# A two-layer f32 decoder trunk on one core: moving the down groups of the two-quarter chunk behind the next up group

## The chip, the cores and the metric

The kernel runs on one core of one Trainium2 chip. The metric is the device time of one execution in microseconds. The kernel before took 2059.43 us (median of 3 runs, 2058.87 to 2060.9).

## What is computed

Two decoder layers on a stream of 256 tokens by 2048 features, all in f32. Layer 0 mixes tokens by causal pooling, layer 1 by dilated attention; both end in a gated feed-forward network (FFN) with a causal convolution of width 3, and that is where the change lies:

```
def conv_ffn(h, w_up, conv_w, conv_b, w_down):
    u = h @ w_up                                   # (256, 2048) @ (2048, 2 * 5504)
    up = jnp.pad(u, ((0, 0), (CONV_WIDTH - 1, 0), (0, 0)))
    c = conv_b + up[:, 0:S] * conv_w[0]
    for j in range(1, CONV_WIDTH):
        c = c + up[:, j:j + S] * conv_w[j]
    gate, val = jnp.split(c, 2, axis=-1)
    return (jax.nn.silu(gate) * val) @ w_down      # (256, 5504) @ (5504, 2048)
...
h = layer_norm(DEEPNORM_ALPHA * h + ff, ln2_g[i], ln2_b[i])
```

## The kernel before

**Units.** Nearly all the work of TensorE (PE) is a list of units. A unit is one block of a weight matrix, 512 x 512 (1 MB) or less. SP loads it into one of 3 `raw` buffers; ScalarE (ACT) casts it to a high part `wh` (L82), and VectorE (DVE) subtracts that from the block to get the low part `wl` (L83); both go into one of 4 buffers. PE then multiplies in three partial products (high by high, high by low, low by high), so that f32 accuracy is kept. `run_units` emits unit after unit: first the loads up to 5 units ahead and the splits up to 3 units ahead, then the matmuls of the unit, then what was put off with `later(n, fn)`, which runs `fn` behind the matmuls of the n-th unit from now. Each engine works through its own queue in this order, so what stands on DVE or ACT in front of a unit's split delays that unit.

**The FFN.** The 5504 inner features are cut into quarters 0 to 10 of 512 (the last one of 384). For each quarter q, `up(q, mid, end)` puts two *up groups* on the list, the gate and the value group, of four units each; `mid` and `end` are lists of units that are put between the two and behind them. After a group its banks are added into `u` (`evac`, L577 and L578), and `conv` makes the three taps: tap 2 with the bias on ACT (L586), then `second` and `third`, each an ACT scaling per block (L591) and a DVE addition (L592), which are put off by one and two units. The gate then gets its SiLU (L615, L616). The value is multiplied in (L670), and one unit later `three` splits the product into the tile `gq[q]` (L287, L283), which the down groups take as left operand.

**Down groups.** Quarters are collected in chunks, (0,1,2), (3,4,5), (6,7), (8,9,10). `down(n)` gives four *column groups* for chunk n, one for each 512 output columns, and each takes one block of weights per quarter. A block is multiplied either with eight products (`go_t`, L235 to L237: 24 matmuls of 512 columns), or, where its quarter is listed in `sevens`, by a Strassen scheme with seven: two units, "a" and "b", of 42 matmuls of 256 columns in all (L224 to L226). A block of seven products needs more from DVE and ACT: the split of the block and of the sums of its parts (`split_sums`, L96 to L109), and once per quarter the sums of the left operand (`left_sums`: L645 to L648, and one unit later L654 and L656). In quarters 2, 5 and 7 these sums take a buffer of the pool `hp`, which has five. The column groups of a chunk are put between the up groups of the next quarters, as `mid` and `end`. `free[q]` and `done[q]` hold unit numbers: `free[9]` is the unit behind which `gq[9]` may be made, since its buffer is one that the two-quarter chunk still reads.

**Behind a column group.** DVE takes the sums of the seven products from their banks (`early_post`, L791 to L798) and adds the rest to `HT[c]`, the residual stream with tokens on partitions (L820, L822); GpSimd (POOL) adds the remaining three pieces by accumulating DMAs (L268).

**The turn.** In layer 0 the last chunk is added with features on partitions (`add_last`), and so `HT[c]` must be turned into `H[c]`: `to_features(c)` transposes 32 x 32 blocks on DVE (L777) into a tile of the pool `hp`, and `moves` places them with 16 DMAs on SP's queue (L767), 6, 5 and 5 of them one, two and three units later. The four turns begin 1, 5, 9 and 13 units after the last column group of chunk 2.

**The end of the FFN.** Behind the value group of quarter 10 come the blocks of quarters 8 and 9 for columns 0, then (`turns`) the block of quarter 8 for columns 1, and only then the block of quarter 10 for columns 0, so that three blocks stand between the end of the value group and the first use of `gq[10]`. In layer 1, quarter 9 takes seven products for columns 0 and 2.

Of the kernel before, what the change touches and what calls it, by code (L numbers as in the profile page):

```python
# [21 lines left out]
NF = FF // P  # L22
# [10 lines left out]
def trunk(ctx: ExitStack, tc: tile.TileContext, x, pool_w_in, pool_w_grp, pool_scale, pool_w_out,  # L33
# [18 lines left out]
    units = []  # L52
    state = {"loaded": 0, "split": 0, "done": 0}
# [66 lines left out]
    def later(n, fn):  # L120
        if n == 0:
            fn()
        else:
            pending.append([n, fn])
# [401 lines left out]
    def add_grp(g):  # L526
# [12 lines left out]
             True, 0, 0, after=lambda q: to_tokens(q))  # L539
# [8 lines left out]
    def ffn(lay):  # L548
# [1 line left out]
        gq, gates, xs = {}, {}, {}  # L550

        chunks = [(0, 3), (3, 6), (6, 8), (8, 11)]
        order = {0: (0, 1, 2), 3: (3, 4, 5), 6: (6, 7), 8: (8, 9, 10)}
        every = (0, 1, 2, 3)
        sevens = {1: every, 2: every, 4: every, 5: every, 6: every, 7: every}
        if lay == 1:
            sevens[9] = (0, 2)
        free, done = {}, {}

        def pads():  # L560
# [4 lines left out]
        def evac(ps, nb, mode):  # L565
            fp = pools["ffn"]
            u = pads()

            def tmp():
                return fp.tile([P, T], F32, name="ut", tag="t1", bufs=4)  # L570

            if mode == "x":
                norm_evac(ps, nb, tmp, lambda m: u[:, m, 2:])
                return u
            for m in range(nb):
                t = tmp()
                A.copy(t, ps[m][:, T:])  # L577
                V.tensor_tensor(u[:, m, 2:], ps[m][:, :T], t, OP.add)  # L578
            return u

        def conv(u, blk0, nb, then):
            cv = cvec[lay]
            c = pools["ffn"].tile([P, 4, T], F32, name="c", tag="t4")
            for m in range(nb):
                j = blk0 + m
                A.activation(c[:, m, :], u[:, m, 2:], AF.Identity, scale=cv[:, 2, j:j + 1], bias=cv[:, 3, j:j + 1])  # L586

            def tap(i, to):
                for m in range(nb):
                    j = blk0 + m  # L590
                    A.activation(to[:, m, :], u[:, m, i:i + T], AF.Copy, scale=cv[:, i, j:j + 1])  # L591
                V.tensor_tensor(c[:, :nb], c[:, :nb], to[:, :nb], OP.add)  # L592

            def second():
                tap(1, pools["ffn"].tile([P, 4, T], F32, name="a", tag="t4"))

            def third():
                tap(0, u[:, :, 0:T])
                then(c)

            later(1, second)
            later(2, third)

        def gate_post(q, nb, mode):
            def post(ps):
# [59 lines left out]
        def val_chain(q, nb, mode, ps):  # L665
            u = evac(ps, nb, mode)

            def valued(c):
                s = gates.pop(q)
                V.tensor_tensor(s[:, :nb], s[:, :nb], c[:, :nb], OP.mult)  # L670

                def three():
                    gq[q] = quad_tile("g")
                    split_act(gq[q], s[:, :nb])
                    if q in sevens:
                        left_sums(q, s)

                at(free.get(q, 0), three)

            after(done.get(q, state["done"] + (0 if q in (2, 5, 10) else 1)), lambda: conv(u, NF + 4 * q, nb, valued))  # L680

        def after(u, fn):
            later(max(u - state["done"], 0), fn)
# [4 lines left out]
        def up(q, mid, end):  # L688
            nb = min(4, NF - 4 * q)
            x0 = q == 0  # L690
            mode = "x" if x0 else "ab"
            group(w_up, rows4, 512 * q, nb * P, psrcs if x0 else xsrcs, gate_post(q, nb, mode),
                  mode=mode)
            for g in mid:
                units.extend(g)
            group(w_up, rows4, FF + 512 * q, nb * P, xsrcs, val_post(q, nb, "ab"))
            for g in end:
                units.extend(g)
# [17 lines left out]
        for n in (0, 1):  # L716
            d = down(n, False)
            q = chunks[n + 1][0]
# [3 lines left out]
            if n == 0:  # L722
                up(q + 2, (), ())
        d = down(2, False)
        up(8, d[:1], d[1:2])
        up(9, d[2:3], d[3:])
        free[9] = len(units) - 1
        up(10, (), ())
        mark = len(units)
        if lay == 0:  # L730
            rows = [(512 * q, min(512, FF - 512 * q)) for q in (8, 9, 10)]
# [12 lines left out]
    def to_tokens(q):  # L744
        if q == 0:
            ST["hb"] = hp.tile([P, 4, T], F32, name="hb", tag="h")
        hb = ST["hb"]
        hf = hb.rearrange("p m t -> p (m t)")
        V.transpose(hf.rearrange("p (t m c) -> p m t c", t=2, m=4), H[q].rearrange("p m (t c) -> p m t c", t=2))

        def to():
            HT[q] = hp.tile([P, 4, T], F32, name="ht", tag="h").rearrange("p a t -> p (a t)").rearrange(
                "p (t c) -> p t c", t=2)
            return HT[q].rearrange("p t c -> p (t c)")

        moves(hf, to)
# [17 lines left out]
    def to_features(c):  # L774
        hb = hp.tile([P, 4, T], F32, name="hb", tag="h")
        hf = hb.rearrange("p m t -> p (m t)")
        V.transpose(hf.rearrange("p (m t c) -> p t m c", m=4, t=2), HT[c].rearrange("p t (m c) -> p t m c", m=4))  # L777

        def to():
            H[c] = hp.tile([P, 4, T], F32, name="h", tag="h")  # L780
            return H[c].rearrange("p m t -> p (m t)")

        moves(hf, to)
# [24 lines left out]
    def tm_post(lay, n, c):  # L808
# [2 lines left out]

        def post(t, ps, half=None):
            y = HT[c][:, t, :]
            if lay == 0 and n == 2 and c == 3 and t == 1:
                for q in range(4):
                    later(1 + 4 * q, lambda q=q: to_features(q))
            if half is None and first:
                V.scalar_tensor_tensor(y, y, ALPHA, ps, op0=OP.mult, op1=OP.add)  # L818
            elif half is None:
                V.tensor_tensor(y, y, ps, OP.add)  # L820
            else:
                V.tensor_tensor(y[:, parts[half]], y[:, parts[half]], ps[:, :256], OP.add)  # L822
            if not last:
                return
            if c == 0 and t == 0:
                ST["bn"] = lnp.tile([P, 2, 8, 6], F32, name="bn", tag="bn")
            for i in range(2) if half is None else (half,):
                V.bn_stats(ST["bn"][:, t, 2 * c + i, :], y[:, parts[i]])
            if c == 2 and t == 1:
                for nm, w in (("g", ln2_g), ("b", ln2_b)):  # L830
                    r = rawp.tile([P, 4, 512], F32, name=nm, tag="raw")
                    nc.sync.dma_start(r.rearrange("p a c -> p (a c)"), w[1:2, :].to_broadcast([P, D]))
                    ST[nm] = r
                later(2, early)
            if c == 3 and t == 0:
                finish0()
            if c == 3 and half == 1:
                finish1()
# [233 lines left out]
    with tc.tile_pool(name="pool", bufs=1) as pp:  # L1072
# [5 lines left out]
        for l in range(2):  # L1078
            n = 80 if l == 0 else 64
# [93 lines left out]
```

## Time and profile before

| | us |
|---|---|
| median of 3 runs | 2059.43 |
| the profiled execution | 2059.19 |
| its span, from the first to the last instruction | 2057.4 |
| PE busy | 2033.1 (99%) |
| DVE busy | 1668.2 (81%) |
| ACT busy | 1242.4 (60%) |

The span is 1.8 us less than the time of the same execution. A PE matmul's duration in the profile is longer than the distance to the next one, since matmuls are pipelined; what a group costs is read from the time between the first matmul of it and the first of the next. A row of the view by windows has, for a stretch of time, its length, the busy time of each engine with the number of instructions that touch the stretch, the mean granted clock (PEclk, 1.00 is full), the DMA share and GB/s.

### The profile page before, as it was taken

To read this page: it belongs to the slowest core of one execution; us is meant where nothing else is said; L and a number is where in the kernel's file an instruction comes from. 1 tells how busy PE (TensorE), PEld (TensorE's weight loads), DVE (VectorE), ACT (ScalarE), POOL (GpSimd) and SP (SyncE) were. 2 spreads that over 40 slices of the span, in tenths; PEclk is the share of its full clock that TensorE was granted. 3 is DMA by queue.
4 is the path that set the end of the run, shared out by engine and by line. 5 is a ranking of instruction groups with operands and counts; after the bars stand their busy time and mean duration, and the time that the engine had idled before them with its cause. 6 is when DMAs were issued, how large, how long until landed. Compare 5 with 4: busy or idle time off the path is not lost. (4 is left out here: it accounts for less than half of the span.)

```text
span 2057.4 us, 30875 instructions
## 1 busy us (share of the span) xinstructions
PE 2033.1 (99%) x12388; PEld 1813.7 (88%) x12388; DVE 1668.2 (81%) x2008; ACT 1242.4 (60%) x1649; POOL 75.2 (4%) x112
## 2 busy tenths in 40 slices
PE   9999999999999989999999999999999999989999
PEld 8899988889889879889888888998898888889987
DVE  6859877988988799789756667787888888889988
ACT  6545687666666566656534444487765676566762
POOL 2000000000000101000000000000001001001000
PEclk9999999999999999999999999999999999999999
DMA  8655567657656657775566555557567647647665
GB/s 260 212 192 185 171 213 209 196 177 233 215 174 203 208 162 228 204 214 183 187 198 194 170 178 168 182 188 223 182 194 230 215 159 222 218 134 226 195 211 177
DMA packets 278304, 405.90 MB, mean 197 GB/s; under 512 B 80414, under 2 KB 95668, under 8 KB 277904
## 3 DMA queue, kind: packets, MB, share of 16 engines
q1 hardware_dynamic: 266144, 389.72, 57.2%
q0 software_dynamic: 11584, 13.55, 4.4%
q8 instruction: 97, 1.59, 0.3%
q10 hardware_dynamic: 432, 0.66, 0.1%
q14 instruction: 47, 0.39, 0.1%
HBM read 380.01 MB, written 2.10 MB: 186 GB/s over the span
## 5 line engine op out<-in xcount | busy, mean ns | idle before, releaser
L165 PE MATMUL acc<-xc,wh 128*128 128x512 f32 x3264 | 1150.2, 396 | 0.0
L166 PE MATMUL acc<-xc,wl 128*128 128x256 f32 x3264 | 917.1, 281 | 0.0
L83 DVE TENSOR_TENSOR wl<-raw,wh 128x2048 fp32r<-128x2048 f32 (+2 forms) x326 | 704.9, 2171 | 235.7 <-ACT wh L82 232.1
L82 ACT CAST wh<-raw 128x2048 fp32r<-128x2048 f32 (+2 forms) x326 | 588.7, 1812 | 275.3 <-PE acc L165 136.6
L165 PEld LDWEIGHTS acc<-xc,wh 128*128 128x128 f32 x3264 | 616.7, 189 | 143.5 <-DVE o L1025 0.6
L166 PEld LDWEIGHTS acc<-xc,wl 128*128 128x128 f32 x3264 | 616.1, 189 | 0.1
L96 ACT CAST wh<-raw 128x1024 fp32r<-128x1024 f32 x100 | 101.3, 1050 | 151.5 <-PE acc L165 57.3
L97 DVE TENSOR_TENSOR wl<-raw,wh 128x1024 fp32r<-128x1024 f32 x100 | 118.5, 1221 | 40.1 <-ACT wh L96 40.1
L103 ACT CAST wh<-raw 128x1024 fp32r<-128x1024 f32 x100 | 78.5, 834 | 42.8 <-PE acc L165 36.6
L577 ACT COPY ut<-acc 128x256 f32<-128x256 f32 x164 | 56.8, 371 | 72.4 <-PE acc L166 72.3
L586 ACT ACTIVATE c<-u,cv 128x256 f32<-128x256 f32 x172 | 89.5, 593 | 13.2 <-DVE f L648 8.2
L106 DVE TENSOR_TENSOR wl<-raw,wh 128x1024 fp32r<-128x1024 f32 x100 | 91.1, 954 | 0.0
L268 POOL DMA_DIRECT2D ht<-w x24 | 20.3, 848 | 1846.9 <-DVE ht L818 1126.5
L226 PE MATMUL t<-wh,g 128*128 128x256 f32 x296 | 84.2, 285 | 3.5 <-DVE u L562 3.5
L225 PE MATMUL t<-wl,g 128*128 128x256 f32 x296 | 84.4, 285 | 0.0
L224 PE MATMUL t<-wh,g 128*128 128x256 f32 x296 | 84.2, 284 | 0.0
L237 PE MATMUL t<-wh,g 128*128 128x512 f32 (+1 forms) x211 | 80.9, 383 | 1.0 <-DVE g L283 1.0
L235 PE MATMUL t<-wh,g 128*128 128x512 f32 (+1 forms) x211 | 81.1, 384 | 0.0
L236 PE MATMUL t<-wl,g 128*128 128x512 f32 (+1 forms) x211 | 80.6, 382 | 0.0
L591 ACT ACTIVATE a<-u,cv 128x256 f32<-128x256 f32 x172 | 73.5, 499 | 7.0 <-DVE g L656 7.0
L225 PE MATMUL s<-wl,xs 128*128 128x256 f32 x252 | 72.0, 286 | 3.9 <-DVE wl L97 3.9
L578 DVE TENSOR_TENSOR u<-acc,ut 128x256 f32<-128x256 f32 x164 | 60.0, 416 | 18.4 <-ACT ut L577 18.4
(274 smaller groups left out, 3473.3 us busy)
## 6 DMA issues: line engine op xcount, KB each, us to landing
raw<-in_ffn_w_up_dram SPq DMA_DIRECT2D x160, 1024.0 KB, 4.9
raw<-in_ffn_w_down_dram SPq DMA_DIRECT2D x80, 1024.0 KB, 5.2
raw<-in_pool_w_out_dram SPq DMA_DIRECT2D x16, 1024.0 KB, 5.0
raw<-in_shared_w_k_dram SPq DMA_DIRECT2D x16, 1024.0 KB, 5.1
raw<-in_attn_w_q_dram SPq DMA_DIRECT2D x16, 1024.0 KB, 5.3
raw<-in_shared_w_v_dram SPq DMA_DIRECT2D x16, 1024.0 KB, 5.7
raw<-in_attn_w_o_dram SPq DMA_DIRECT2D x16, 1024.0 KB, 5.0
raw<-in_pool_w_in_dram SPq DMA_DIRECT2D x12, 1024.0 KB, 5.3
```

Source lines behind the costliest of these rows:

```text
L82: A.copy(wh[i][:, s], r[:, s])
L83: V.tensor_tensor(wl[i][:, s], r[:, s], wh[i][:, s].bitcast(F32), OP.subtract)
L96: A.copy(h[:, :, n], r[:, :, n])
L97: V.tensor_tensor(l[:, :, n], r[:, :, n], h[:, :, n].bitcast(F32), OP.subtract)
L106: V.tensor_tensor(l[:, k, n], r[:, k, n], h[:, k, n].bitcast(F32), OP.subtract)
L165: PE.matmul(ps[m], h[:, k, c], q[:, k, :, :T], start=st, stop=False)
L166: PE.matmul(ps[m][:, :T], l[:, k, c], q[:, k, 0, :T], start=False, stop=sp and not shifted)
L224: PE.matmul(to, xh, h[:, k, n], start=opens and kk == 0, stop=False)
L225: PE.matmul(to, xh, l[:, k, n], start=False, stop=False)
L226: PE.matmul(to, xl, h[:, k, n], start=False, stop=ends and kk == 1)
L235: PE.matmul(to, xh, h[:, k, c], start=j == 0 and k == 0, stop=False)
L586: A.activation(c[:, m, :], u[:, m, 2:], AF.Identity, scale=cv[:, 2, j:j + 1], bias=cv[:, 3, j:j + 1])
```

## The change

- In both layers the four column groups of chunk 2 (quarters 6 and 7) are placed later: behind the value group of quarter 8 instead of behind its gate group, and so on, the last one between the gate and the value group of quarter 10 instead of behind quarter 9. `free[9]` moves with the last of them.
- In layer 0 quarter 7 takes eight products instead of seven, and comes first in each column group of its chunk.
- In layer 0 the turn of each column `c` begins three units after its own column group.
- The value of quarter 10, in both layers, gets its second and third tap at once instead of one and two units later.

```
-        order = {0: (0, 1, 2), 3: (3, 4, 5), 6: (6, 7), 8: (8, 9, 10)}
+        order = {0: (0, 1, 2), 3: (3, 4, 5), 6: (6, 7) if lay == 1 else (7, 6), 8: (8, 9, 10)}
         every = (0, 1, 2, 3)
-        sevens = {1: every, 2: every, 4: every, 5: every, 6: every, 7: every}
+        sevens = {1: every, 2: every, 4: every, 5: every, 6: every}
         if lay == 1:
-            sevens[9] = (0, 2)
+            sevens.update({7: every, 9: (0, 2)})
...
-        def conv(u, blk0, nb, then):
+        def conv(u, blk0, nb, then, quick=False):
...
-            later(1, second)
-            later(2, third)
+            for n, fn in ((1, second), (2, third)):
+                later(0 if quick else n, fn)
...
-            after(done.get(q, state["done"] + (0 if q in (2, 5, 10) else 1)), lambda: conv(u, NF + 4 * q, nb, valued))
+            after(done.get(q, state["done"] + (0 if q in (2, 5, 10) else 1)), lambda: conv(u, NF + 4 * q, nb, valued, q == 10))
...
         d = down(2, False)
-        up(8, d[:1], d[1:2])
-        up(9, d[2:3], d[3:])
-        free[9] = len(units) - 1
-        up(10, (), ())
+        up(8, (), d[:1])
+        up(9, d[1:2], d[2:3])
+        up(10, d[3:], ())
+        free[9] = len(units) - 5
...
-            if lay == 0 and n == 2 and c == 3 and t == 1:
-                for q in range(4):
-                    later(1 + 4 * q, lambda q=q: to_features(q))
+            if lay == 0 and n == 2 and t == 1:
+                later(3, lambda: to_features(c))
```

How the change moves instructions is shown at three places on DVE. The digits in a name are buffer numbers; the number behind `wl`, `wh` and `raw` is that of the unit. From line 816 on, line numbers are one less in the changed program.

**Layer 0, where the first column group of chunk 2 is prepared.** `c_6327` is the gate of quarter 7 and `g_...` its `gq[7]`. Before:

```order
L592 TENSOR_TENSOR c_6804<-c_6804,u_6630 128x1024
L670 TENSOR_TENSOR c_6327<-c_6327,c_6804 128x1024
L97 TENSOR_TENSOR wl145_6925<-raw144_6764,wh145_6924 128x4x256 x2
L283 TENSOR_TENSOR g_6962<-c_6327,g_6962 128x4x256
L645 TENSOR_TENSOR f_6968<-c_6327 128x256
L646 TENSOR_TENSOR f_6968<-f_6968,c_6327 128x256
L647 TENSOR_TENSOR f_6968<-c_6327 128x256
L648 TENSOR_TENSOR f_6968<-c_6327,f_6968 128x256
L104 TENSOR_TENSOR raw146_6874<-raw146_6874 128x2x256
L106 TENSOR_TENSOR wl146_6976<-raw146_6874,wh146_6975 128x4x256
```

And changed:

```order
L592 TENSOR_TENSOR c_6804<-c_6804,u_6630 128x1024
L670 TENSOR_TENSOR c_6327<-c_6327,c_6804 128x1024
L83 TENSOR_TENSOR wl145_6923<-raw145_6822,wh145_6922 128x2048
L283 TENSOR_TENSOR g_6958<-c_6327,g_6958 128x4x256
L83 TENSOR_TENSOR wl146_6964<-raw146_6876,wh146_6963 128x2048
L562 MEMSET u_6999 128x4x2
L578 TENSOR_TENSOR u_6999<-acc_6828,ut_7001 128x256
L578 TENSOR_TENSOR u_6999<-acc_6829,ut_7004 128x256
L578 TENSOR_TENSOR u_6999<-acc_6830,ut_7007 128x256
L578 TENSOR_TENSOR u_6999<-acc_6831,ut_7010 128x256
L83 TENSOR_TENSOR wl147_7016<-raw147_6920,wh147_7015 128x2048
L83 TENSOR_TENSOR wl148_7061<-raw148_6961,wh148_7060 128x2048
```

Units 144 to 147 were the column group (two blocks of seven products each), split around the making of `gq[7]`; now they are the value group of quarter 8, with plain splits, the left sums of quarter 7 are gone, and the column group begins with unit 148.

**Layer 1, behind the value group of quarter 10.** `u_18651` and `u_18517` are that group's `u`; the `L97` of the first row ends the split of quarter 9's block for columns 0; `wl403` and `wl399` belong to the block of quarter 8 for columns 1, `wl404` and `wl400` to that of quarter 10 for columns 0. Before:

```order
L97 TENSOR_TENSOR wl402_18620<-raw401_18507,wh402_18619 128x4x256 x2
L616 TENSOR_TENSOR c_18540<-u_18496,c_18540 128x768
L562 MEMSET u_18651 128x4x2
L578 TENSOR_TENSOR u_18651<-acc_18513,ut_18653 128x256
L578 TENSOR_TENSOR u_18651<-acc_18514,ut_18656 128x256
L578 TENSOR_TENSOR u_18651<-acc_18515,ut_18659 128x256
L83 TENSOR_TENSOR wl403_18669<-raw403_18577,wh403_18668 128x2048
L592 TENSOR_TENSOR c_18662<-c_18662,a_18698 128x768
L83 TENSOR_TENSOR wl404_18706<-raw404_18617,wh404_18705 128x1536
L592 TENSOR_TENSOR c_18662<-c_18662,u_18651 128x768
L670 TENSOR_TENSOR c_18540<-c_18540,c_18662 128x768
```

And changed:

```order
L97 TENSOR_TENSOR wl398_18488<-raw397_18382,wh398_18487 128x4x256 x2
L562 MEMSET u_18517 128x4x2
L578 TENSOR_TENSOR u_18517<-acc_18388,ut_18519 128x256
L578 TENSOR_TENSOR u_18517<-acc_18389,ut_18522 128x256
L578 TENSOR_TENSOR u_18517<-acc_18390,ut_18525 128x256
L592 TENSOR_TENSOR c_18528<-c_18528,a_18532 128x768
L592 TENSOR_TENSOR c_18528<-c_18528,u_18517 128x768
L670 TENSOR_TENSOR c_18258<-c_18258,c_18528 128x768
L83 TENSOR_TENSOR wl399_18545<-raw399_18449,wh399_18544 128x2048
L283 TENSOR_TENSOR g_18574<-c_18258,g_18574 128x3x256
L83 TENSOR_TENSOR wl400_18580<-raw400_18485,wh400_18579 128x1536
```

The taps and the product moved ahead of the two splits.

**Layer 0, the first turn.** `ht_2837` is `HT[0]`. Before, it stands among the splits of quarter 10's up groups:

```order
L820 TENSOR_TENSOR ht_3471<-ht_3471,t0_8022 128x512
L822 TENSOR_TENSOR ht_3471<-ht_3471,t1_8023 128x256
L83 TENSOR_TENSOR wl175_8164<-raw175_8085,wh175_8163 128x1536
L777 STREAM_TRANSPOSE hb_8194<-ht_2837 128x2x4x128
L83 TENSOR_TENSOR wl176_8199<-raw176_8115,wh176_8198 128x1536
```

And changed:

```order
L107 TENSOR_TENSOR raw156_7325<-raw156_7325 128x2x256
L108 TENSOR_TENSOR raw156_7325<-raw156_7325 128x2x256
L109 TENSOR_TENSOR raw156_7325<-raw156_7325 128x2x256
L777 STREAM_TRANSPOSE hb_7450<-ht_2837 128x2x4x128
L97 TENSOR_TENSOR wl157_7455<-raw156_7325,wh157_7454 128x4x256 x2
```

It now stands one column group after its own, inside the split of the next group's seven-product block.

## The prediction

> **What bounds the kernel now.** I read the page first, then who waits for whom on PE, then the view by windows at each place where PE waits.
>
> ```profile
> span 2057.4 us, 30875 instructions
> PE 2033.1 (99%) x12388; PEld 1813.7 (88%) x12388; DVE 1668.2 (81%) x2008; ACT 1242.4 (60%) x1649; POOL 75.2 (4%) x112
> ```
>
> ```profile
> PE s L225 <- DVE wl L106: 4.8, 2, 2.4
> PE s L225 <- DVE wl L97: 3.9, 4, 1.6
> PE acc L165 <- DVE g L283: 3.7, 1, 3.7
> PE t L226 <- DVE u L562: 3.5, 2, 2.1
> PE t L237 <- DVE g L283: 1.0, 1, 1.0
> ```
>
> PE sets the end: it is busy nearly throughout, and an engine of 81% can only cost time where PE has to wait for it. The waits inside the program are these five rows (us in total, times, longest), and the releaser is DVE in all of them. Where do they lie? The windows below run from the first matmul of a group to the first of the next, except the last four.
>
> ```profile
> 686.75:692.34 5.59, 5.59 (x26) 4.52 (x25) 4.76 (x7) 1.84 (x3) 0.00 (x0) 1.00 0.41 157
> 702.24:724.72 22.48, 22.48 (x130) 19.64 (x129) 17.13 (x24) 13.33 (x23) 2.58 (x3) 1.00 0.62 180
> 724.72:743.83 19.11, 12.24 (x87) 11.42 (x85) 18.30 (x27) 13.80 (x23) 0.00 (x0) 0.91 0.26 85
> 766.31:776.22 9.91, 9.91 (x86) 9.91 (x85) 8.53 (x13) 9.71 (x14) 0.00 (x0) 1.00 0.46 158
> 841.00:906.97 65.97, 62.25 (x346) 54.09 (x345) 50.83 (x53) 35.70 (x44) 2.58 (x3) 0.97 0.84 236
> 1835.88:1855.60 19.72, 14.34 (x87) 13.34 (x86) 18.91 (x27) 14.43 (x23) 0.00 (x0) 0.74 0.30 99
> 1878.07:1887.97 9.90, 9.90 (x86) 9.90 (x85) 7.77 (x11) 9.70 (x14) 0.00 (x0) 1.00 0.37 122
> 1952.72:1986.46 33.74, 33.74 (x194) 29.51 (x193) 27.87 (x35) 20.56 (x29) 2.58 (x3) 1.00 0.76 241
> ...
> 739.19:742.60 3.41, 2.86 (x13) 2.86 (x14) 2.73 (x3) 3.41 (x6) 0.00 (x0) 0.50 0.17 43
> 892.78:896.19 3.41, 0.69 (x4) 0.61 (x5) 3.25 (x4) 2.63 (x2) 0.00 (x0) 1.00 0.84 238
> 896.19:899.60 3.41, 3.41 (x13) 2.92 (x12) 2.88 (x4) 0.00 (x0) 0.00 (x0) 0.50 0.98 270
> 2002.80:2004.20 1.40, 0.39 (x2) 0.00 (x0) 1.40 (x3) 0.81 (x1) 0.00 (x0) 1.00 0.60 230
> ```
>
> A column group of two seven-product blocks takes 9.91 us (84 matmuls; a window's count has those at its edges too), except the first of chunk 2 in each layer: 19.11 and 19.72 us, where DVE is busy 18.3 and 18.9 us. A block of eight products takes 5.59 us, an up group 22.48 us, that is 22.48 / 64 = 0.351 us for each pair of a 512 and a 256 column matmul. The stretch from 841.00 has quarter 10's two groups (2 x 4 x 12 pairs) and the first five blocks behind them (16, 16, 16, 12, 16), 172 pairs or 60.42 us, and took 65.97: 5.55 too long. The clock is part of all this: behind a wait it stood at 0.50 for 3.4 us, or, in 1835.88 to 1855.60, for longer (mean 0.74).
>
> **Part 1: the column groups of chunk 2 begin an up group later.** What makes the first of them late is DVE's queue:
>
> ```profile
> 726.58 2.35 DVE L97 TENSOR_TENSOR wl<-raw,wh 128x1024 fp32r<-128x1024 f32 x2
> 728.86 1.22 DVE L283 TENSOR_TENSOR g<-c,g 128x1024 fp32r<-128x1024 f32 x1
> ...
> 731.46 0.69 DVE L104 TENSOR_TENSOR raw<-raw 128x512 f32<-128x512 f32 x1
> ...
> 735.25 0.69 DVE L109 TENSOR_TENSOR raw<-raw 128x512 f32<-128x512 f32 x1
> 735.86 0.69 DVE L656 TENSOR_TENSOR xs<-f,xs 128x512 fp32r<-128x512 f32 x1
> ...
> 737.48 1.08 DVE L578 TENSOR_TENSOR u<-acc,ut 128x256 f32<-128x256 f32 x3
> 738.47 2.35 DVE L97 TENSOR_TENSOR wl<-raw,wh 128x1024 fp32r<-128x1024 f32 x2
> ```
>
> From 726.58 to 740.82 it is back to back: splitting a block of seven (L104 to L109 with L97, some 6.8 us from 731.46), making `gq[7]` with its sums (2.6 us from 728.86, 1.3 us from 735.86), adding up the gate of quarter 8, all in the 9.9 us that PE needs. With the up group in front, the making of `gq[7]` falls beside 22.5 us of PE work whose four plain splits take 4 x 2.2 us of DVE. I add DVE's work in that group for layer 1: splits of its last unit and of the three pieces ahead 2.2 + 4.5 + 2.3 + 4.5, additions, product and sums of banks 4.8, together 18.3 of 22.5 us. So DVE gains 4 us there and adds to its lead, the time between the end of a split and PE's use of it. Both first groups come down to what the others take. Layer 1: 19.72 - 9.90 = 9.82 us gained. Layer 0 has the other block type: 19.11 - (5.59 + 9.91 / 2) = 8.57 gained.
>
> Behind them the pattern "value group, column group, gate group, column group" is that of before, shifted, where no row waits. New is the last place, between the two short groups of quarter 10: 33.74 / 2 = 16.87 us each. A cycle of one short group and one column group gives PE 26.8 us. DVE's work in it is, from a full cycle of before:
>
> ```profile
> 1920.38:1952.72 32.34, 32.34 (x214) 29.54 (x213) 29.91 (x35) 22.25 (x34) 2.59 (x3) 1.00 0.65 195
> ```
>
> 29.9 us less a quarter of four splits (4 x 0.54, from 2.29 and 1.75 us for blocks of 2048 and 1536) and of the tap work (about 1.2) is 26.5 us: as much as PE has. That holds without a wait only because DVE begins ahead; one short cycle takes from the lead rather than adding the 2.4 us of a full one. I put it at nothing. If the lead doesn't suffice, each of some six units is late by up to 1 us.
>
> **Part 2: quarter 7 in layer 0 with eight products.** PE pays 5.59 - 4.95 = 0.64 us per block. The first column group has it above; three more make +1.92. DVE has one plain subtraction of 2.29 us instead of 6.8, and no left sums: cover for part 3.
>
> **Part 3: the turn behind each group.** No PE work. Four transposes (1.24 us) move into DVE's queue ahead of the L97 of a seven-product block, and with each 16 DMAs on SP (some 0.6 us each to issue) ahead of weight loads. What can hold them is the accumulation into `HT[c]`:
>
> ```profile
> 754.50 0.85 POOL L268 DMA_DIRECT2D ht<-w  x1 [38.59 <-ACT wh L103]
> 755.03 2.05 POOL L268 DMA_DIRECT2D ht<-u  x2
> ...
> 760.81 2.43 DVE L97 TENSOR_TENSOR wl<-raw,wh 128x1024 fp32r<-128x1024 f32 x2
> ```
>
> ```profile
> DMA to landing us min/median/max: 3.3/4.7/8.5
> ...
>   DMA h<-hb: 4.9, 2
> ```
>
> The first rows are the timeline, the others the views of lines L268 and L777.
>
> Here the column group ended at 743.83, POOL issued from 754.50 to 757.1, and a median landing is at 762, 18 us after the end. DVE reaches the turn no sooner than the buffer of the split ahead comes free, two units (11.2 us) after the end, plus 4.5 us of that split, so 15.7 us: it would stand about 2 us. In this row the L97 was done at 763.2 and PE used it from 768.5, 5 us later, and the plain block of quarter 7 adds to that. I cost the part at nothing; without that cover it is some 2 us per column. It takes away the 4.9 us that DVE waited for one turn's DMAs before the next.
>
> **Part 4: the taps of quarter 10 at once.** In layer 0 this removes the 5.55 us: three blocks, 16.8 us, follow the group, and the chain of copies, taps, product and split needs about 9 us now that nothing stands between. In layer 1 it removes the 1.0 us at 2002.80, but the chain now stands ahead of the split of quarter 8's block for columns 1:
>
> ```profile
> 1987.38 2.35 DVE L97 TENSOR_TENSOR wl<-raw,wh 128x1024 fp32r<-128x1024 f32 x2
> 1989.65 0.95 DVE L616 TENSOR_TENSOR c<-u,c 128x768 f32<-128x768 f32 x1
> 1990.54 0.41 DVE L578 TENSOR_TENSOR u<-acc,ut 128x256 f32<-128x256 f32 x1
> ...
> 1994.40 2.29 DVE L83 TENSOR_TENSOR wl<-raw,wh 128x2048 fp32r<-128x2048 f32 x1 [2.79 <-ACT wh L82]
> ```
>
> ```profile
> 1990.98 1.59 ACT L586 ACTIVATE c<-u,cv 128x256 f32<-128x256 f32 x3 [1.75 <-DVE u L578]
> 1992.48 1.89 ACT L82 CAST wh<-raw 128x2048 fp32r<-128x2048 f32 x1
> 1994.27 1.31 ACT L591 ACTIVATE a<-u,cv 128x256 f32<-128x256 f32 x3
> 1995.48 1.47 ACT L82 CAST wh<-raw 128x1536 fp32r<-128x1536 f32 x1
> ```
>
> Before, that block's `wl` was done 6.15 us after the first L578 (1996.69 less 1990.54), and PE used it at 1997.2. Two tap rounds on ACT, 1.21 us each (1994.27 to 1995.48), now come before its cast: 8.6 us. The group ended at 1986.46 and the block is due 5.59 + 4.95 us later, its `wl` at 10.8. The first L578 stood at 4.1; without L616 (now earlier) 3.2, which makes PE wait 1.0 us. But the sums of quarter 9 (3.9 us of DVE) move from quarter 10's gate group into its value group; if none of it is absorbed, the L578 stands at 7.1 and the wait is 4.9. I take a third of that, 4.5, since this group has the lead of a plain stretch: a wait of 2.4 us.
>
> **The sum.** Layer 0: -8.57 + 1.92 - 5.55 = -12.2. Layer 1: -9.82 - 1.0 + 2.4 = -8.4. Together -20.6: the profiled execution's 2059.19 us becomes 2038.6. It lies 0.2 us under the median, so the forecast against the runs is **2038.8 us**.
>
> **The clock.** In 892.78 to 896.19 PE was busy 0.69 of 3.41 us, and the next 3.41 us ran at 0.50; the 1.0 us wait at 2002.80 left the clock at 1.00. So a wait of about 2.7 us inside one such window is enough, and costs 1.7 us more. [...]
>
> **The rivals.**
> - *No new wait in layer 1.* The lead absorbs the chain: 2.4 us less, 2036.4. For it: the block was in time before by 0.5 us. Against it: 2.4 us more of ACT work ahead of its cast.
> - *The long wait in layer 1.* Nothing of quarter 9's sums is absorbed: 4.9 us and 1.7 for the clock, 2038.8 + 4.2 = 2043.0. For it: the 26.5 of 26.8 us just before.
> - *DVE becomes the bound around the last column group*, in both layers: six units late by up to 1 us in layer 1, half of this in layer 0, and the clock twice: 2038.8 + 9 + 3.4 = 2051. Against it: leads of several us in the rows of before.
> - *The waits only move*: the first column groups still find DVE behind, and stand at 19 us. The gain is then part 4 less part 2, 1 to 4 us: 2055 to 2059. Against it: the 18.3 of 22.5 us.
> - *The turns hold DVE*, slower. The place is L777 ahead of the L97. It decides when the accumulation lands so late that the lead is used up: about 2 us of standing, plus 5 of lead at each column. To lose the 12.2 us of layer 0 and 8.4 of layer 1, each of four holds has to cost PE over 5.2 us, so land 10 us later than the median. With 6.5 us each, 26 in all: 2064. For it: DVE works in order, and SP's loads queue behind the turn's DMAs too. Against it: the largest landing is 8.5 us, 3.8 over the median.
>
> **How the numbers follow.** Forecast 0.50 (2036.5 to 2041), no new wait 0.13, long wait 0.15, DVE the bound 0.10, waits move 0.05, turns hold 0.07. Below the forecast only the first rival lies, less about 1.5 us of spread: 2034.5. Upward the range takes the long wait and half of the DVE case: 2047. 0.2% is 4.1 us, about what a measurement of this kernel can tell from no change. Faster are the first four and half of the fifth, 0.89; the same the other half, 0.03; slower the last, and a small part for what I do not see, 0.08.
>
> **What would show it.** Right: the first column group of chunk 2 takes 10.5 us in layer 0 and 9.9 in layer 1 with PEclk 1.00; the other three of layer 0 take 10.5; no wait of `acc` for `g`; one wait of PE in layer 1 for the `wl` of L83 behind quarter 9's first block, 1 to 5 us. Wrong: a wait for L97 behind a transpose, waits for `wl` in quarter 10's groups, or a clock of 0.50 in the FFNs. The prediction fails as a whole if the lead of DVE in the value group of quarter 8 doesn't form.

## The result and the profile after

| | before | changed |
|---|---|---|
| median of the runs, us | 2059.15 (2056.26 to 2060.9, 4 runs) | 2041.12 (2040.18 to 2042.79, 4 runs) |
| span of the profiled execution, us | 2057.4 | 2041.0 |
| mean granted clock | 0.995 | 0.998 |

The ratio is 0.9915, with a 95% interval of 0.9898 to 0.9932: the changed kernel is faster by 18.0 us in the medians. The page of its profile and PE's waits (us in total, times, longest):

```profile
span 2041.0 us, 30664 instructions
PE 2029.8 (99%) x12316; PEld 1805.3 (88%) x12316; DVE 1648.8 (81%) x1973; ACT 1235.0 (61%) x1634; POOL 75.2 (4%) x112
```

```profile
PE t L236 <- DVE wl L83: 1.9, 1, 1.9
PE acc L168 <- ACT wh L82: 1.8, 1, 1.8
...
PE t L235 <- ACT wh L82: 0.8, 1, 0.8
...
PE acc L166 <- DVE wl L83: 0.4, 1, 0.4
```

All five rows of before are gone, those for `g` among them. The L168 row lies at 8 us, in the start of the kernel, which the change does not touch; it is 1.8 us here, between 0.2 and 1.6 in some of the kernels below and absent in others. The other three rows are layer 1. The places of the prediction in the view by windows (length, then busy PE, PEld, DVE, ACT, POOL, then PEclk, DMA share, GB/s):

```profile
748.35:758.86 10.51, 10.51 (x68) 9.46 (x67) 6.88 (x9) 8.89 (x12) 0.00 (x0) 1.00 0.61 201
841.72:852.23 10.51, 10.51 (x69) 9.46 (x67) 7.24 (x10) 7.91 (x11) 0.00 (x0) 1.00 0.67 156
852.23:895.79 43.56, 43.56 (x250) 38.05 (x249) 34.27 (x38) 24.01 (x28) 2.58 (x3) 1.00 0.86 256
1847.21:1857.13 9.92, 9.92 (x86) 9.92 (x85) 9.16 (x14) 8.29 (x15) 0.00 (x0) 1.00 0.29 94
1857.13:1880.34 23.21, 22.79 (x130) 19.64 (x129) 22.98 (x25) 14.24 (x19) 2.59 (x3) 1.00 0.79 244
1966.35:1977.88 11.53, 10.71 (x68) 9.42 (x66) 8.99 (x14) 8.70 (x15) 0.00 (x0) 1.00 0.58 204
1977.88:2006.82 28.94, 27.05 (x108) 21.56 (x109) 27.39 (x33) 12.83 (x11) 0.00 (x0) 0.94 0.58 200
```

**Layer 0.** The first two rows are the first and the last column group of chunk 2: 10.51 us each, with PE busy from end to end. The third row is the stretch from the last column group to the end of the fifth block behind quarter 10, without a wait. Against before, the first column group is worth 10.51 - 19.11 = -8.60, the other three 3 x (10.51 - 9.91) = +1.8, and the wait for `gq[10]` -5.55: 12.3 us less.

**Layer 1.** The fourth row is the first column group, 9.92 us in place of 19.72: -9.80. The gate group of quarter 9 behind it (fifth row) takes 23.21 in place of 22.48: +0.7, the 0.4 of L166 in the waits. The 1.0 us wait for `gq[10]` is gone. The last two rows hold the new wait: the first blocks of quarters 8 and 9 behind the value group of quarter 10 take 11.53 us in place of 5.59 + 9.91 / 2 = 10.54, since PE stops at their end for the `wh` of quarter 8's block for columns 1 (the 0.8 of L235); then it waits for that block's `wl` and runs at a mean clock of 0.94. The same stretch of PE's work takes 25.11 us in a kernel below that has no wait there. So this place costs 1.0 + 3.8 = 4.8 us. Layer 1 gains 9.80 - 0.7 + 1.0 - 4.8 = 5.3 us.

Together 12.3 + 5.3 = 17.6, less 1.1 us by which the FFN of layer 0 began later in this execution (the start of the kernel): 16.5 against the 16.4 us between the two spans. The profiled execution of the changed kernel is the longest of its four (2042.79 us), so the spans show 1.6 us less gain than the medians.

### The profile page after: what moved, and what is told of

It reads as the page before. It is cut to its first block, busy times and chain, and to the rows that moved or that the text cites. A ratio compares the mean times of both kernels' runs of the same rounds, so it can differ in the third digit from the quotient of the medians.

```text
span 2041.0 us, 30664 instructions
## 1 busy us (share of the span) xinstructions
PE 2029.8 (99%) x12316; PEld 1805.3 (88%) x12316; DVE 1648.8 (81%) x1973; ACT 1235.0 (61%) x1634; POOL 75.2 (4%) x112
## 5 line engine op out<-in xcount | busy, mean ns | idle before, releaser
L166 PE MATMUL acc<-xc,wl 128*128 128x256 f32 x3264 | 915.9, 281 | 0.4 <-DVE wl L83 0.4
L83 DVE TENSOR_TENSOR wl<-raw,wh 128x2048 fp32r<-128x2048 f32 (+2 forms) x330 | 713.8, 2171 | 238.8 <-ACT wh L82 233.0
L82 ACT CAST wh<-raw 128x2048 fp32r<-128x2048 f32 (+2 forms) x330 | 596.5, 1814 | 279.7 <-PE acc L165 136.5
L166 PEld LDWEIGHTS acc<-xc,wl 128*128 128x128 f32 x3264 | 615.4, 189 | 0.9 <-DVE wl L83 0.7
L96 ACT CAST wh<-raw 128x1024 fp32r<-128x1024 f32 x92 | 93.3, 1050 | 146.5 <-PE acc L165 69.4
L97 DVE TENSOR_TENSOR wl<-raw,wh 128x1024 fp32r<-128x1024 f32 x92 | 108.8, 1219 | 38.6 <-ACT wh L96 38.5
L103 ACT CAST wh<-raw 128x1024 fp32r<-128x1024 f32 x92 | 72.2, 834 | 49.8 <-PE acc L165 42.9
L236 PE MATMUL t<-wl,g 128*128 128x512 f32 (+1 forms) x243 | 93.9, 387 | 1.9 <-DVE wl L83 1.9
L235 PE MATMUL t<-wh,g 128*128 128x512 f32 (+1 forms) x243 | 94.6, 389 | 0.8 <-ACT wh L82 0.8
L237 PE MATMUL t<-wh,g 128*128 128x512 f32 (+1 forms) x243 | 94.0, 387 | 0.0
L106 DVE TENSOR_TENSOR wl<-raw,wh 128x1024 fp32r<-128x1024 f32 x92 | 83.7, 951 | 0.2 <-ACT wh L103 0.2
L578 DVE TENSOR_TENSOR u<-acc,ut 128x256 f32<-128x256 f32 x164 | 60.2, 414 | 21.0 <-ACT ut L577 21.0
L225 PE MATMUL t<-wl,g 128*128 128x256 f32 x272 | 76.4, 281 | 0.0
L224 PE MATMUL t<-wh,g 128*128 128x256 f32 x272 | 76.4, 281 | 0.0
L226 PE MATMUL t<-wh,g 128*128 128x256 f32 x272 | 76.3, 281 | 0.0
L591 ACT ACTIVATE u<-u,cv 128x256 f32<-128x256 f32 x172 | 73.4, 499 | 0.0
```

The source lines that it names most:

```text
L82: A.copy(wh[i][:, s], r[:, s])
L83: V.tensor_tensor(wl[i][:, s], r[:, s], wh[i][:, s].bitcast(F32), OP.subtract)
L96: A.copy(h[:, :, n], r[:, :, n])
L97: V.tensor_tensor(l[:, :, n], r[:, :, n], h[:, :, n].bitcast(F32), OP.subtract)
L106: V.tensor_tensor(l[:, k, n], r[:, k, n], h[:, k, n].bitcast(F32), OP.subtract)
L166: PE.matmul(ps[m][:, :T], l[:, k, c], q[:, k, 0, :T], start=False, stop=sp and not shifted)
```

## The experiments

Medians are set against runs of the kernel before on the same chip; ratios have 95% intervals. "Part" is one of the four parts of the prediction. Lines of diffs are against the kernel that the text names.

**Part 4 alone: the taps of quarter 10 at once, everything else as before.** Against the kernel before:

```
-            later(1, second)
-            later(2, third)
+            for n, fn in ((1, second), (2, third)):
+                later(0 if quick else n, fn)
...
-conv(u, NF + 4 * q, nb, valued))
+conv(u, NF + 4 * q, nb, valued, q == 10))
```

> The kernel before with part 4 alone: the value of quarter 10 gets its second and third tap at once, in both layers; column groups, quarter 7 and turns as before. Theory (each part works by itself; in layer 1 the taps ahead of the split of quarter 8's block for columns 1 are what makes that block late, by 8.6 us from the first L578 to its wl): layer 0 loses its 5.55 us; in layer 1 the first L578 stands some 4.1 us behind the value group, as before, so the block is ready at 12.7 against 10.8 us, a wait of 1.9 us in the place of the 1.0 us for g; in all 2059.2 - 5.5 + 0.9 = 2054.6 us. Rival (the new wait in layer 1 comes from the moved sums of quarter 9 and the short groups, not from the taps): no wait there, 2059.2 - 5.5 - 1.0 = 2052.7 us, and PE has no wait behind quarter 10 in either layer.

Measured: 2055.22 us (9 runs) against 2060.03, ratio 0.9978 [0.9968, 0.9988]. PE's waits:

```profile
PE s L225 <- DVE wl L106: 4.8, 2, 2.4
...
PE t L236 <- DVE wl L83: 1.7, 1, 1.7
...
PE shift L362 <- DVE S L345: 0.9, 1, 0.9
```

Both waits for `gq[10]` are gone and the first column groups are as late as before (L106). The wait for `wl` in layer 1 is there without the other parts: the three taps ahead of the split make it. It is 1.7 us here and, with all four parts, 1.9 behind a stop of 0.8 for `wh`. The prediction's reason for a longer one, the sums of quarter 9 that part 1 moves into quarter 10's value group, fits that: the first L578 stands 3.96 us behind the group here (1986.91 less 1982.95) and 5.25 us with all four parts. In layer 1 the two kernels differ in part 1 alone, but no run has the sums by themselves. The L362 row is new too: the last split ahead of DVE's sums for the norm waits 1.70 us for ACT's cast. Why the cast is late there was not tested.

**Part 1 alone: the column groups of chunk 2 an up group later.** Against the kernel before:

```
-        up(8, d[:1], d[1:2])
-        up(9, d[2:3], d[3:])
-        free[9] = len(units) - 1
-        up(10, (), ())
+        up(8, (), d[:1])
+        up(9, d[1:2], d[2:3])
+        up(10, d[3:], ())
+        free[9] = len(units) - 5
```

> The kernel before with part 1 alone: the column groups of chunk 2 an up group later in both layers; quarter 7 of layer 0 with seven products, turns and taps as before. Theory: the first column group takes 9.9 to 10.6 us in both layers (8.5 to 9.2 us gained in layer 0, about 9.1 in layer 1), while the wait for the g of quarter 10 stays and grows by 1 to 2 us in each layer because the sums of quarter 9 now lie in its value group: 2059.2 - 9 - 9.1 + 3 = about 2044 us. Rival (without the eight products of quarter 7, DVE is behind in layer 0): the column groups of layer 0 stand at 12 us and more with waits for L97, and the time is 2049 us or more.

Measured: 2051.42 us (4 runs), ratio 0.9955 [0.9941, 0.997]. The number is the rival's, but not by its mechanism: each of the eight column groups takes 9.9 us. PE's waits and the DVE row behind the first of them:

```profile
PE acc L399 <- DVE S L348: 5.1, 1, 5.1
PE acc L165 <- DVE g L283: 4.7, 1, 4.7
PE t L237 <- DVE g L283: 1.4, 1, 1.4
```

```profile
944.57 1.42 DVE L318 TENSOR_TENSOR h<-h,acc 128x256 f32<-128x256 f32 x4 [4.95 <-DMA h<-hb]
```

The two waits for `gq[10]` stay, as they must without part 4. The first row is new: before, the four turns ran from the last column group through quarter 10's up groups; now that the last column group comes later, the fourth turn (13 units behind it) ends inside the last chunk. DVE stands 4.95 us for its DMAs before it can add to `H[3]`, and the sums for the norm (`S`) and PE's use of them (L399) wait in turn. In the view by windows the stretch from the block in which PE stops to the end of the chunk is

```profile
936.69:969.27 32.58, 27.19 (x199) 26.09 (x198) 26.30 (x31) 18.49 (x24) 0.00 (x0) 0.90 0.48 155
```

The changed kernel needs 5.75 + 18.29 = 24.04 us for it (its rows stand with the next run), 8.5 less. That is most of what part 1 alone gives back of its gain.

**Part 3 undone: the turns spread as before, behind the last column group.** Against the changed kernel:

```
-            if lay == 0 and n == 2 and t == 1:
-                later(3, lambda: to_features(c))
+            if lay == 0 and n == 2 and c == 3 and t == 1:
+                for q in range(4):
+                    later(1 + 4 * q, lambda q=q: to_features(q))
```

> The changed kernel with part 3 alone undone: the four turns of layer 0 start 1, 5, 9 and 13 units after the last column group again. Theory (part 3 has a price only together with part 1: with the column groups later, turns counted from the last of them end inside the last chunk): the DMAs of the fourth turn land after quarter 10's last block is done, DVE stands for them, and PE waits for the sums of the layer norm (L399 for S) by 5 us or more, then runs at half clock for 3.4 us; the column groups and quarter 10 in layer 0 are as in the changed kernel. 2041.1 + 8.7 (what the same place lost with part 1 alone) = 2050 us, up to 2055. Rival (the prediction as it was costed: part 3 is free either way): 2041 us, and no wait for S.

Measured: 2047.28 us (4 runs) against 2059.18, ratio 0.9949 [0.9935, 0.9964]: 6.2 us over the changed kernel. PE's waits, windows (the block of the last chunk where PE stops, and what follows), and DVE:

```profile
PE acc L399 <- DVE S L348: 4.3, 1, 4.3
```

```profile
930.91:941.09 10.18, 5.91 (x50) 5.70 (x49) 7.01 (x14) 2.28 (x5) 0.00 (x0) 1.00 0.71 222
941.09:963.06 21.97, 21.21 (x149) 20.57 (x150) 20.74 (x21) 16.52 (x21) 0.00 (x0) 0.84 0.40 133
```

```profile
914.68 1.25 DVE L777 STREAM_TRANSPOSE hb<-ht 128x1024 f32<-128x1024 f32 x1 [1.15 <-DMA h<-hb]
...
937.97 1.42 DVE L318 TENSOR_TENSOR h<-h,acc 128x256 f32<-128x256 f32 x4 [3.07 <-DMA h<-hb]
```

and the same stretch of the changed kernel:

```profile
932.61:938.36 5.75, 5.75 (x51) 5.75 (x50) 5.58 (x11) 3.37 (x8) 0.00 (x0) 1.00 0.89 322
938.36:956.65 18.29, 18.29 (x151) 17.99 (x149) 17.16 (x17) 13.75 (x17) 0.00 (x0) 1.00 0.39 122
```

10.18 + 21.97 against 5.75 + 18.29: 8.1 us at this one place, with a clock of 0.84 in the second stretch. The mechanism is the theory's; the median is 2.7 us under its 2050, and the rival without a wait for `S` fell. The last turn begins at 914.68, and DVE has its DMAs at 937.97, 23 us later. This execution is the longest of the four (2050.47 us), and part of the 8.1 may be its own. So part 3 is worth 6.2 us in the medians once part 1 is made, by a place at the very end of the layer.

**Parts 2 and 3 undone: quarter 7 of layer 0 with seven products, the turns as before.** Against the kernel with part 3 undone, above:

```
-        order = {0: (0, 1, 2), 3: (3, 4, 5), 6: (6, 7) if lay == 1 else (7, 6), 8: (8, 9, 10)}
+        order = {0: (0, 1, 2), 3: (3, 4, 5), 6: (6, 7), 8: (8, 9, 10)}
...
-        sevens = {1: every, 2: every, 4: every, 5: every, 6: every}
+        sevens = {1: every, 2: every, 4: every, 5: every, 6: every, 7: every}
...
-            sevens.update({7: every, 9: (0, 2)})
+            sevens[9] = (0, 2)
```

> The changed kernel with parts 2 and 3 undone (quarter 7 of layer 0 has seven products again; the four turns come 1, 5, 9 and 13 units behind the last column group of chunk 2, as before the change); parts 1 and 4 stay. To be set beside the run with part 3 alone undone (2047.28 us), which differs from it in quarter 7 only, and beside the run with the turns three units apart (2063.01), which differs in the distance of the turns only. Theory: eight products in quarter 7 cost PE 4 x 0.6 us and are worth only the cover that they give; with the turns four units apart nothing needs it but the first column group's 0.8 us wait, so this is 2047.3 - 2.5 + 0.8 = 2045.6 us, the four column groups of layer 0 take 9.9 us, and the wait for S in the last chunk stays. The loss of the other run then came from the distance of the turns alone: there DVE stood 7.05 and 6.59 us for one turn's DMAs ahead of the next one's transpose. Rival: the blocks of seven leave DVE without a lead for the taps of quarter 10, whose product is then late whatever the turns do: 2049 us or more, with a wait of acc for g in layer 0.

Measured: 2047.8 us (2044.72 to 2050.35, 6 runs) against 2060.01, ratio 0.9938 [0.9926, 0.995]. The four column groups take 9.9 us, and no wait for `g` is left: the rival's mechanism fell. The waits:

```profile
PE acc L399 <- DVE S L348: 4.4, 1, 4.4
...
PE acc L166 <- DVE wl L83: 1.1, 2, 0.5
...
PE shift L362 <- DVE S L345: 0.9, 1, 0.9
```

Of the 2.5 us that the seven products save, some 0.5 go to a wait behind the first column group (one of the two in the second row; the other is layer 1's) and 0.9 to the wait at L362, which the theory left out. At L362 the last split ahead of the sums for the norm again waits for ACT's cast (1.63 us); the run with part 3 alone undone has the same turns and no such wait, so what makes it is open. In the runs the two kernels can't be told apart: with the turns as before, part 2 is worth nothing that could be measured.

**The same with the turns three units apart**, beginning 1, 4, 7 and 10 units behind the last column group (`1 + 3 * q` in the line above), so that they end sooner.

> The changed kernel with quarter 7 of layer 0 at seven products again, in the old order (6, 7); since its sums then hold the fifth buffer until the last column group, the turns start after that group, 1, 4, 7 and 10 units behind it. Theory (the eight products are there to free the buffer, not to spare DVE): column groups 9.9 us instead of 10.5, 2.6 us less for PE, with a wait of 0.4 to 1 us behind the first group as in layer 1; the turns, three units apart, make DVE stand for the DMAs of the one before, which gives back 1 to 6 us, and PE doesn't wait for S at the end: 2040 to 2045 us. Rival (DVE needs the relief): the column groups of layer 0 take 11 us or more with waits for wl, and the time is over 2046 us.

Measured: 2063.01 us (9 runs), ratio 1.0019 [1.0008, 1.0029]: 15.2 us more than with four units, and the theory's number fell. The time is the rival's, but its mechanism isn't: the column groups of layer 0 take 9.9 us here too. PE's waits and DVE:

```profile
PE shift L362 <- DVE S L345: 8.4, 1, 8.4
PE acc L399 <- DVE S L348: 3.0, 1, 3.0
PE acc L165 <- DVE u L578: 2.3, 1, 2.3
...
PE acc L165 <- DVE g L283: 1.5, 1, 1.5
```

```profile
858.79 1.24 DVE L777 STREAM_TRANSPOSE hb<-ht 128x1024 f32<-128x1024 f32 x1
...
877.55 1.25 DVE L777 STREAM_TRANSPOSE hb<-ht 128x1024 f32<-128x1024 f32 x1 [7.05 <-DMA h<-hb]
...
898.40 1.25 DVE L777 STREAM_TRANSPOSE hb<-ht 128x1024 f32<-128x1024 f32 x1 [6.59 <-DMA h<-hb]
...
916.59 1.25 DVE L777 STREAM_TRANSPOSE hb<-ht 128x1024 f32<-128x1024 f32 x1 [6.18 <-DMA raw<-in_ffn_w_down_dram]
```

The last five DMAs of the first of these turns, in SP's timeline:

```profile
871.07 3.26 SPq L767 DMA_DIRECT2D h<-hb  x5
```

This third part goes out until 874.3, three units behind the turn, and the next transpose, three units on, must wait until it has landed (1.9 to 6.7 us from issue to landing for these DMAs, median 4.3). DVE works in order and stands 7.05 and 6.59 us. Ahead of the fourth transpose it stands another 6.18; the view puts that down to a weight load, which SP issued (912.55) right behind the third turn's last DMAs (until 912.46). Everything behind these transposes is late: the sums of banks (L578), the making of `gq[10]` (L283), the additions for the norm (8.4 us of PE at L362). Four units left 4.9 us of standing in two waits in the kernel before and one wait of 1.5 us in the run above, which differs from this one in nothing else. An up group between two turns, as in the changed kernel, leaves one of 2.6:

```profile
  DMA ht<-u: 2.6, 1
```

This is the view of the transposes (L777) of the changed kernel; what it waits for there is the accumulation into `HT[c]`, and no row names the DMAs from `hb`. The rival of the prediction in which the turns hold DVE is thus real, at another place: it is the distance between two turns that decides, not the landing of the accumulation.

**Layer 1 with the taps of quarter 10 spread as before** (part 4 in layer 0 alone). Against the changed kernel:

```
-conv(u, NF + 4 * q, nb, valued, q == 10))
+conv(u, NF + 4 * q, nb, valued, q == 10 and lay == 0))
```

> The changed kernel, but in layer 1 the taps of quarter 10 come one and two units later again; layer 0 as changed. Theory: the wait for quarter 8's block for columns 1 (1.0 us for wh, 2.1 for wl, and 3.4 us at half clock, 4.8 in all) goes, since cast and split stand ahead of the taps again: 0.7 us of wait for that wl at most, and the wait for the g of quarter 10 comes back at 1 to 2.5 us, so 2041.1 - 4.8 + 2.5 = 2038.8 us (2037 to 2040). Rival (DVE is the bound around the short groups): the block of quarter 8 still waits 2 us or more, and with the g wait the time is 2041 us or more.

Measured: 2038.28 us (4 runs), ratio 0.9895 [0.9878, 0.9912], against 0.9915 of the changed kernel. PE's waits:

```profile
PE t L237 <- DVE g L283: 1.4, 1, 1.4
...
PE t L236 <- DVE wl L83: 0.6, 1, 0.6
```

As the theory had it: two waits of 1.4 and 0.6 us at full clock (the mean over the execution is 1.000) in place of 2.7 us and half clock. By the medians part 4 thus costs 2.8 us more in layer 1 than the wait that it removes; the intervals of the two ratios overlap from 0.9898 to 0.9912, and the waits and the clock are the better evidence.

**Layer 1 with the three taps at once, but one unit later.** Against the changed kernel:

```
-            after(done.get(q, state["done"] + (0 if q in (2, 5, 10) else 1)),
+            after(done.get(q, state["done"] + (0 if q in (2, 5) or q == 10 and lay == 0 else 1)),
```

> The changed kernel, but in layer 1 all three taps of quarter 10 stand one unit later, at once, so behind the split of quarter 8's block for columns 1. Theory: the split is done about 4 us earlier than in the changed kernel and that wait of 4.8 us is gone; g of quarter 10 is made about 14 us behind the value group and is due at 16.1, so no wait: 2036.3 us. Rival (the g chain is then too late): a wait of 2 to 4 us for g of quarter 10, 2039 to 2041 us.

Measured: 2036.89 us (2036.44 to 2038.25, 4 runs), ratio 0.9887 [0.9872, 0.9902]. The only wait for a split left in PE's list, and the window of the 108 matmuls:

```profile
PE acc L166 <- DVE wl L83: 0.6, 1, 0.6
```

```profile
1976.51:2001.62 25.11, 25.11 (x110) 20.28 (x109) 24.47 (x30) 12.73 (x12) 0.00 (x0) 1.00 0.59 189
```

The taps now stand behind the split of quarter 8's block for columns 1 and ahead of quarter 10's own; both are in time. Of the kernels here this has the lowest median, 4.2 us under the changed kernel; by the ratios it is 0.28% faster, with intervals that overlap by 0.0004.

**The same, with the value of quarter 8 taken from its banks one unit later** in layer 1, aimed at the 0.6 us behind the first column group. Against the kernel above:

```
-later(1 if q == 0 else 0, lambda: val_chain
+later(1 if q == 0 or q == 8 and lay == 1 else 0, lambda: val_chain
```

> The changed kernel with, in layer 1, all three taps of quarter 10 one unit later (as in l1_conv_later) and the value of quarter 8 taken from its banks one unit later. Theory: the wait of 0.7 us behind the first column group of layer 1 comes from DVE's 1.4 us of that value ahead of the last split of the group; moved behind it, the wait is gone, and no wait of PE for a split is left in the FFNs: 2036.9 - 0.7 = 2036.2 us. Rival (DVE simply has too much work there): the wait stays at 0.7 us, 2036.9 us.

Measured: 2037.12 us (4 runs), ratio 0.9898 [0.9883, 0.9912], the same as without it. The theory's 2036.2 us fell, and the rival's 2036.9 came. The windows are the gate group of quarter 9, behind the first column group, and its value group, behind the second.

```profile
1854.35:1876.94 22.59, 22.59 (x131) 19.68 (x129) 21.53 (x24) 14.79 (x22) 2.59 (x3) 1.00 0.77 228
1886.86:1910.08 23.22, 22.80 (x131) 19.68 (x129) 22.99 (x25) 14.44 (x19) 2.58 (x3) 1.00 0.81 243
```

The wait left the first place and appeared at the second, behind the next column group, where DVE has 22.99 us of work in 23.22 and the first split waits 1.29 us for ACT's cast. It only moved; by the medians the two kernels can't be told apart.

What was not tried: parts 1, 3 and 4 with seven products in quarter 7, since its sums hold the fifth buffer of `hp` that an early turn needs.

## Why the prediction came out as it did

- **Layer 0 was right to the term.** Forecast -8.57, +1.92 and -5.55, measured -8.60, +1.8 and -5.55. The reason held too: with the move alone, without the other parts, the column groups come down to 9.9 us, and with part 4 alone the wait for `gq[10]` goes.
- **Layer 1's column group was right**, 9.92 us, but the group behind it was taken as free of waits and has 0.7 us. DVE's queue there, in the changed kernel:

```profile
1850.09 1.22 DVE L616 TENSOR_TENSOR c<-u,c 128x1024 f32<-128x1024 f32 x1
1851.24 0.41 DVE L578 TENSOR_TENSOR u<-acc,ut 128x256 f32<-128x256 f32 x1
...
1852.56 2.35 DVE L97 TENSOR_TENSOR wl<-raw,wh 128x1024 fp32r<-128x1024 f32 x2
1855.61 2.29 DVE L83 TENSOR_TENSOR wl<-raw,wh 128x2048 fp32r<-128x2048 f32 x1 [0.69 <-ACT wh L82]
```

  The value group of quarter 8 now ends just before the column group, so its sums of banks and the SiLU's product stand ahead of the last L97 of that column group and of the split that follows. ACT is in the chain too: its tap waits for DVE's sums and stands ahead of the cast for which that split waits 0.69 us.

```profile
1851.69 2.09 ACT L586 ACTIVATE c<-u,cv 128x256 f32<-128x256 f32 x4 [0.43 <-DVE u L578]
```

  The prediction said that the pattern behind the first column group is that of before, shifted, where no row waits; it did not count what is new ahead of the first one. Its count of DVE's work in the value group of quarter 8, 18.3 of 22.5 us, came out at 22.38:

```profile
1824.73:1847.21 22.48, 22.48 (x130) 19.64 (x129) 22.38 (x29) 18.74 (x31) 0.00 (x0) 1.00 0.59 194
```

  Three plain splits (L83, 2.3 us each) fall into it where the count has one, "its last unit". The column group itself has PE busy throughout, so the lead formed; that it grew by 4 us is not borne out.
- **The new wait in layer 1 was mis-sized: 2.4 us forecast, 4.8 measured.** The place and the chain were right. (By the prediction's own figures, 4.5 + 8.6 - 10.8, the wait is 2.3.) The row of DVE where the prediction put the first L578 at 4.5 us, and the split of the block:

```profile
1971.60 0.41 DVE L578 TENSOR_TENSOR u<-acc,ut 128x256 f32<-128x256 f32 x1
...
1977.93 2.28 DVE L83 TENSOR_TENSOR wl<-raw,wh 128x2048 fp32r<-128x2048 f32 x1
```

  The group ended at 1966.35, so the L578 stands at 5.25 us, and the `wl` is done at 1980.21, 8.6 us behind it as forecast. PE's rows of waits give 0.8 + 1.9 = 2.7 us where the sum has 2.4. What was mis-sized is mostly the clock: the prediction adds nothing for it at its wait of 2.4 us, and here it stood at half for 3.4 us (the last section), 1.7 us more. The remaining 0.4 of the 4.8 us these rows don't resolve. The step that fell short is thus the term `+2.4` of the sum, which should have had the 1.7 for the clock with it. A clock of 0.50 in the FFNs was one of the prediction's own signs of being wrong, and it came; no wait for L97 behind a transpose did, and none for `wl` within quarter 10's groups.
- **Part 3 was mis-priced.** "I cost the part at nothing" is right for the turns themselves (DVE stands 2.6 us once; about 2 were forecast for each column) but the step left out what part 1 does to the old turns: they would end in the last chunk. The 6.2 us that this saves are in no term of the sum; the total still came out, because the loss was left out as well as its remedy. That the two cancel was luck, since the prediction saw neither.
- **Part 2 as cover** was right in kind: without it, and with the old turns, waits of 0.5 and 0.9 us stand in layer 0 and use up some of what seven products save. Whether its plain blocks are needed as cover for part 3 was not shown, since part 3 was not tried without them.
- **The rivals.** Neither the case without a new wait nor the waits that only move held; DVE did not become the bound around the last column group, neither in layer 0 (7.24 of 10.51 us) nor in layer 1, where the short group and the column group took 26.80 us with PE busy throughout and DVE 25.80. The long wait of layer 1 was half right: it had 4.9 us and 1.7 for the clock, 6.6 together, against the 4.8 measured; the clock fell as it said, but the wait was 2.7 us. Its 2043.0 lies about as far above the median as the forecast lies below it. Turns that hold DVE cost PE time only where they are set three units apart, or where part 1 stands without part 3.
- **The forecast**, 2038.8, lies 2.3 us under the median. By the spans 20.6 us were forecast and 16.4 measured; the 4.2 are 3.1 in layer 1 and the 1.1 at the start of the kernel, which is no part of the change.

## What to carry to other kernels

Before moving a group of work, list what is scheduled relative to it, and ask where that ends now; part 1 alone gained 8.6 us here, and a large part of its gain came only with the remedy for the part that was carried along. Work placed ahead of a split in the same engine's queue should be set between two splits that have lead, not moved as far forward as possible: by the medians one unit later was 4.2 us better than at once. Where one step refills a buffer that the DMAs of the step before still read, set the two further apart than the last issue plus its landing: four units instead of three were 15.2 us better.

## What the runs showed of the hardware

The clock of PE fell to half after a stretch in which PE was not idle throughout. In the changed kernel:

```profile
1977.53:1980.94 3.41, 1.17 (x4) 0.77 (x5) 3.41 (x3) 3.19 (x4) 0.00 (x0) 1.00 0.00 0
1980.94:1984.35 3.41, 3.41 (x10) 2.66 (x9) 3.41 (x3) 1.39 (x2) 0.00 (x0) 0.50 0.78 262
```

PE was busy 1.17 of 3.41 us, with two waits and a matmul between them, and the next 3.41 us ran at 0.50. The prediction took 2.7 us of waiting as what is needed; here 2.2 us within one such stretch (3.41 less 1.17) came ahead of the slow one.

In the kernel before, slow stretches begin at 739.18, 896.19 and 1845.10, 157.01 and 948.91 us apart, which is 46 and 278 times 3.413 us. In steps of that length, the stretches ahead of the first and the third are the last two rows here; the first row, with PE busy 1.80 us, is followed by the second at full clock. The one ahead of 896.19 stands in the prediction, with 0.69 us.

```profile
732.35:735.77 3.42, 1.80 (x13) 1.59 (x13) 3.35 (x5) 1.92 (x5) 0.00 (x0) 1.00 0.26 95
735.77:739.18 3.41, 0.86 (x5) 0.65 (x5) 3.41 (x10) 2.63 (x5) 0.00 (x0) 1.00 0.00 0
...
1841.69:1845.10 3.41, 1.04 (x9) 0.83 (x8) 3.38 (x7) 2.32 (x7) 0.00 (x0) 1.00 0.73 272
```

Two more cases are both behind quarter 10 in layer 1, in the run with part 3 undone (first row, followed by a clock of 0.50) and in the run with part 4 alone (second row, followed by 1.00):

```profile
1982.66:1986.07 3.41, 1.45 (x10) 0.94 (x8) 3.38 (x3) 3.19 (x3) 0.00 (x0) 1.00 0.01 2
1992.51:1995.92 3.41, 1.69 (x12) 1.34 (x11) 3.41 (x3) 3.20 (x4) 0.00 (x0) 1.00 0.00 0
```

So in these rows a slow stretch came behind 0.69, 0.86, 1.04, 1.17 and 1.45 us of PE, and full clock behind 1.69 and 1.80. Behind 1845.10 the clock of the kernel before stayed at 0.50 for three steps:

```profile
1845.10:1848.51 3.41, 2.00 (x10) 1.71 (x9) 3.38 (x9) 2.09 (x2) 0.00 (x0) 0.50 0.02 5
1848.51:1851.93 3.42, 2.38 (x10) 2.09 (x11) 3.29 (x6) 3.35 (x5) 0.00 (x0) 0.50 0.00 0
1851.93:1855.34 3.41, 3.41 (x18) 3.41 (x17) 2.86 (x2) 3.41 (x6) 0.00 (x0) 0.50 0.70 229
```

At 739.18 and 896.19 PE was busy 2.86 and 3.41 us in the slow stretch, and full clock followed. These are single cases; what the clock goes by was not tested.
